# Dividing attention outputs by the softmax sums, and spreading the mLSTM's stabiliser rows by DMA: one encoder layer on one core

## The chip, the cores and the metric

One of the eight cores of a Trainium2 chip runs the kernel. The metric is the device time of one execution in microseconds (us); lower is better. The core has five engines, each with an instruction queue of its own: TensorE (PE, matmuls and transposes), VectorE (DVE), ScalarE (ACT), GpSimd (POOL) and SyncE (SP, which here only issues transfers, in order). Transfers themselves run on 16 DMA engines.

## What is computed

One layer of a hybrid encoder, applied to two groups of 512 tokens (width 1024) with shared weights. The parts that matter here:

```python
# mLSTM, per head and direction (stabiliser m_comb, one value per token)
m_comb = jnp.maximum(d_inter, jnp.max(d_intra, axis=-1))
w_intra = jnp.exp(d_intra - m_comb[..., None])
s = jnp.einsum('bhtd,bhsd->bhts', qb, kb) * w_intra
...
h = num / jnp.maximum(jnp.abs(den), jnp.exp(-m_comb))[..., None]
# attention, 8 heads
scale = (A_NOPE + A_ROPE) ** -0.5
s = jnp.einsum('bqhd,bkhd->bhqk', qn, k_nope) + jnp.einsum('bqhr,bkr->bhqk', qr, k_rope)
p = jax.nn.softmax(s.astype(jnp.float32) * scale, axis=-1).astype(v.dtype)
return jnp.einsum('bhqk,bkhd->bqhd', p, v)
```

Around them stand RMS norms, one input projection, merge gates, two branch projections, an output projection, a SwiGLU feed-forward part and a gated embedding.

## The kernel before

Activations lie transposed: 128 channels on the partitions, the 512 tokens of one group (g = 0, 1) along a row. Nearly every product is made of three matmuls of high and low parts (hi*hi, hi*lo, lo*hi); a tensor is split by a cast (ACT, line 158 or 168) and a subtraction (line 154). Weights come in by SP: load, split, use, through two buffers of each kind.

Order of the work: each engine has a queue, and a scheduler with a timing model chooses the order of the instructions from the code as it is written, by their dependences and free buffers. Some stretches are pinned to program order; those that the change touches are not. So a changed instruction can move others.

**The mLSTM stage** (about 80 to 490 us of the profile). A function `mlstm_proj` (line 515) makes queries, keys, values and output gates of a head; `mlstm_chain` (line 584) does one head and one group in two directions (d = 0, 1), 16 directions in all. The stabiliser, with sign turned, is kept for all 64 rows (direction, group, head) in `Mn`, one row of 512 tokens each; `nmr` stacks its high and low parts (lines 495 and 496). For one direction the row is needed on all 128 partitions: POOL casts a column of `esel` to a selection matrix `sel` (line 594), one matmul spreads the row into the PSUM bank `b0` (line 596), and two more make `b1`, the same with the causal mask added (lines 598 and 599). Ten Exp per direction (line 611) read blocks of `b0`, and of `b1` where the block lies on the diagonal, with a bias per partition. The result is multiplied by the scores (line 619) and split (lines 620 and 154); the products with the values (line 633) follow, then the division and the norm. Banks of PSUM in this stage: two for projections (`mm`), two for scores and products, two for transposes, two shared by `b0`, `b1` and another spread (`bc`).

**Merge gates** (line 695) and the values of attention (lines 720 to 734) follow, some gates also between heads of attention.

**Attention** (about 600 to 861 us): for each of 8 heads and 2 groups, `attn_proj` (line 773) makes the operands, reading the values `avt` from DRAM (line 787), and `attn` (line 791) works in four blocks of 128 queries. A block has five score matmuls (lines 799 to 803) into a bank of `sc` (three banks), the maximum over keys (DVE, line 805), its multiplication by -scale (DVE, line 806), Exp with that bias and the sum over keys as a second output (ACT, line 808), the sum's reciprocal (DVE, line 809), the normalising of p (line 811 on ACT for three blocks, line 813 on DVE for one), four transposes into a bank of `pt` (line 816, two banks), and the split of the result (line 818 on ACT, line 154 on DVE, into `aph` and `apl`). After the four blocks twelve matmuls with the values fill the one bank of `av` (lines 823 to 825); ACT copies it to `oz` (line 827, pool EV, tag "ch", two buffers), and SP stores it in DRAM (line 828).

**Hops**: between the last heads, the operands of the next stage (the projection of the mLSTM's outputs, lines 956 to 958) are loaded from DRAM (line 832), summed on POOL or DVE (lines 862 to 875, `ld`), and split (line 884 for the cast, `xh`). `HOPS` (line 1435) says how many units are written behind which head. When the last head begins, loads go to other buffers for a second pass of sums. The pool EV with tag "bk" (two buffers) holds the merge gates' rows `tg` and a part of the hops' loads.

**Behind 861 us**: branch projections, output projection, feed-forward and embedding, untouched by the change.

## Time and profile before

| | |
|---|---|
| runs | 1882.21, 1882.19, 1881.48 us |
| median of the runs | 1882.19 us |
| span of the profiled execution | 1884.6 us (2.4 us above the median) |
| TensorE, busy | 1846.2 us, 98% |
| VectorE, ScalarE, GpSimd, busy | 1234.4, 885.5, 374.5 us |
| granted TensorE clock, mean | 0.993 of full speed |

How rows are read: a group's row has line, engine, operation, out<-in by the program's names, shapes and count, then busy time in us and the mean of one in ns, then the idle time of the engine just before these instructions with what ended it. A row of the timeline begins with the start and the duration in us. "PE sc L799 <- ACT p L808: 4.5, 5, 2.4" means that TensorE, before the instruction of line 799, waited for ACT's line 808: 4.5 us in total, five times, 2.4 us at the longest. Matmuls are pipelined, so the records of two neighbours overlap; the distance between their starts is what one costs.

### The profile page before, as it was taken

How to read it: one execution, taken by the hardware profiler on the slowest of the kernel's cores; microseconds unless marked ns; L12 is line 12 of the kernel's file. 1: busy time of each engine (PE TensorE's matmuls, PEld its weight loads, DVE VectorE, ACT ScalarE, POOL GpSimd, SP SyncE). 2: the span in 40 equal slices, each digit the busy share in tenths (PEclk: the TensorE clock that was granted, in tenths of full speed). 3: DMA queues.
4: the chain of work that ended last, by engine and by line, in shares of the span. 5: the costliest groups of instructions: out<-in, count | busy, mean ns of one | idle time of the engine just before them, and what ended most of it. 6: DMA issues, size and time to landing. Idle time of an engine off the chain costs nothing.

```text
span 1884.6 us, 24479 instructions
## 1 busy us (share of the span) xinstructions
PE 1846.2 (98%) x8849; PEld 1535.3 (81%) x8849; DVE 1234.4 (66%) x2200; ACT 885.5 (47%) x1726; POOL 374.5 (20%) x281
## 2 busy tenths in 40 slices
PE   9999999999999999899999999999999999999996
PEld 7888898988887888677878888888888887888786
DVE  6747575836554667976897587444444568878756
ACT  6255465543444666775434355333433343434333
POOL 0000000100000000352050003665566523111000
PEclk9999999999999999999999999999999999999998
DMA  4111111112254222445565241332223346543332
GB/s 166 52 45 35 57 34 57 35 67 71 81 170 140 65 73 87 129 153 192 166 207 173 90 162 68 111 118 95 95 90 121 103 158 228 157 130 100 106 134 95
DMA packets 98377, 208.11 MB, mean 110 GB/s; under 512 B 10832, under 2 KB 21456, under 8 KB 98256
## 3 DMA queue, kind: packets, MB, share of 16 engines
q1 hardware_dynamic: 85600, 161.72, 25.8%
q10 hardware_dynamic: 12096, 43.00, 7.1%
q0 software_dynamic: 560, 1.84, 0.2%
q8 instruction: 69, 1.13, 0.2%
q14 instruction: 52, 0.43, 0.1%
HBM read 151.89 MB, written 54.10 MB: 109 GB/s over the span
## 4 chain that ended last, share of the span: by engine, by line
PE 85%; DVE 9%; DMA 3%; ACT 1%; issue 1%; SPq 0%; POOL 0%; ACTq 0%; DVEq 0%
PE b L956 13%; PE b L958 12%; PE b L957 12%; PE mm L183 7%; PE mm L185 7%; PE mm L184 7%; PE mm L79 3%; PE nm L633 3%; DVE xl L154 2%; PE mm L548 2%; PE mm L550 2%; PE mm L549 2%; PE pt L816 1%; PE mm L1322 1%; PE mm L1323 1%
## 5 line engine op out<-in xcount | busy, mean ns | idle before, releaser
L957 PE MATMUL b<-xl,wp 128*128 128x512 f32 x1148 | 448.1, 392 | 1.7 <-DVE xl L154 1.7
L956 PE MATMUL b<-xh,wp 128*128 128x512 f32 x1148 | 442.1, 393 | 6.6 <-ACT u L997 2.3
L958 PE MATMUL b<-xh,wp 128*128 128x512 f32 x1148 | 444.2, 392 | 0.4 <-DVE wp L154 0.4
L900 ACT CAST wp<-wst 128x512 fp32r<-128x512 f32 (+1 forms) x270 | 164.2, 612 | 307.3 <-PE b L958 258.9
L154 DVE TENSOR_TENSOR wp<-wst,wp 128x512 fp32r<-128x512 f32 (+1 forms) x270 | 235.6, 875 | 67.0 <-ACT wp L900 66.6
L956 PEld LDWEIGHTS b<-xh,wp 128*128 128x128 f32 x1148 | 216.1, 188 | 59.1 <-ACT wp L900 5.5
L957 PEld LDWEIGHTS b<-xl,wp 128*128 128x128 f32 x1148 | 216.0, 188 | 49.0 <-DVE xl L154 2.6
L958 PEld LDWEIGHTS b<-xh,wp 128*128 128x128 f32 x1148 | 215.8, 188 | 48.3 <-DVE wp L154 1.3
L183 PE MATMUL mm<-hh,whi 128*128 128x512 f32 x560 | 220.4, 394 | 0.6 <-ACT raw L79 0.3
L184 PE MATMUL mm<-hl,whi 128*128 128x512 f32 x560 | 219.5, 392 | 0.0
L185 PE MATMUL mm<-hh,wlo 128*128 128x512 f32 x560 | 219.3, 392 | 0.0
L1002 DVE TENSOR_TENSOR u<-b,u 128x512 f32<-128x512 f32 x90 | 61.7, 689 | 132.5 <-PE b L958 82.6
L168 ACT CAST whi<-wst 128x1024 fp32r<-128x1024 f32 (+1 forms) x69 | 71.0, 1029 | 114.4 <-PE mm L184 69.6
L183 PEld LDWEIGHTS mm<-hh,whi 128*128 128x128 f32 x560 | 105.6, 189 | 23.3 <-ACT raw L79 0.8
L185 PEld LDWEIGHTS mm<-hh,wlo 128*128 128x128 f32 x560 | 105.5, 188 | 21.9
L184 PEld LDWEIGHTS mm<-hl,whi 128*128 128x128 f32 x560 | 105.6, 189 | 21.4
L927 POOL TENSOR_TENSOR s<-wst,wst 128x512 f32<-128x512 f32 (+1 forms) x30 | 47.4, 1579 | 321.9 <-DMA wst<-w 87.3
L154 DVE TENSOR_TENSOR wlo<-wst,whi 128x1024 fp32r<-128x1024 f32 (+1 forms) x69 | 83.1, 1204 | 30.9 <-ACT whi L168 30.5
L997 ACT COPY u<-b 128x512 f32<-128x512 f32 x90 | 50.8, 589 | 98.0 <-PE b L958 70.7
L1220 POOL TENSOR_TENSOR sg<-sg,u 128x512 f32<-128x512 f32 x30 | 54.6, 1819 | 203.3 <-DVE u L1002 203.3
L154 DVE TENSOR_TENSOR xl<-ld,xh 128x512 fp32r<-128x512 f32 x121 | 89.1, 764 | 7.0 <-ACT xh L884 6.2
L154 POOL TENSOR_TENSOR vnl<-avt,vnh 128x512 fp32r<-128x512 f32 x16 | 21.2, 1322 | 309.9 <-ACT vnh L158 251.4
(357 smaller groups left out, 3621.4 us busy)
## 6 DMA issues: line engine op xcount, KB each, us to landing
wst<-w SPq DMA_DIRECT2D x73, 512.0 KB
wst<-w ACTq DMA_DIRECT2D x60, 512.0 KB
ld<-actd SPq DMA_DIRECT2D x77, 256.0 KB
actd<-t SPq DMA_DIRECT2D x40, 256.0 KB
x<-x SPq DMA_DIRECT2D x32, 256.0 KB
ld<-hzd SPq DMA_DIRECT2D x32, 256.0 KB
wst<-wd ACTq DMA_DIRECT2D x16, 512.0 KB
actd<-sg SPq DMA_DIRECT2D x30, 256.0 KB
```

Of the source, the lines that this page charges most:

```text
L79: r = f(*args, **kw)
L154: e.tensor_tensor(out=out, in0=src, in1=hi.bitcast(F32), op=ALU.subtract)
L168: S.copy(hi[:, :n], st[:, :n])
L183: E.matmul(bk, whi[:, c], hi, start=k == 0, stop=False)
L184: E.matmul(bk, whi[:, c], lo, start=False, stop=False)
L185: last_mm[0] = E.matmul(bk, wlo[:, c], hi, start=False, stop=k == nk - 1)
L633: E.matmul(bk, l, r, start=n == 0, stop=n == len(terms) - 1)
L900: S.copy(hi, src)
L956: E.matmul(bk, whi[:, c], hi, start=bool(first) and k == 0, stop=False, **sk)
L957: E.matmul(bk, whi[:, c], lo, start=False, stop=False, **sk)
L958: E.matmul(bk, wlo[:, c], hi, start=False, stop=k == self.kh - 1, **sk)
L1002: V.tensor_tensor(out=t, in0=b, in1=t, op=ALU.add if name == "P2" else ALU.subtract)
```

## The change

*mLSTM.* `nmr`, `esel`, `sel` and the three matmuls per direction go. `Mn` is written once to DRAM (`nmd`); for each direction SP loads one row of it, broadcast to 128 partitions, into `b0`, a buffer of pool EV with tag "bk" (256 KB); POOL adds the mask into `b1`, a buffer of pool MC (two). The Exps read SBUF in place of PSUM, the masks stay fp32, and one of the two `bc` banks becomes a third `mm` bank.

*Attention.* The scale goes into the norm of the query latent (`lat_norms`), the maximum comes out negated, and Exp takes it as its bias; lines 806, 811 and 813 go. The four sums of a head's blocks stand in one tile `den`; one reciprocal makes `rden` (128x4). That is written to DRAM transposed, in pieces of one element (`rsd`), read back broadcast to 128 partitions into `rb` (pool EV, tag "bk"), and POOL multiplies `oz` by it before it is stored. Probabilities stay undivided up to there.

By count, in the instruction queues: PE 48 fewer (the matmuls); DVE 132 fewer (64 scalings, 48 reciprocals, 16 normalising passes, 4 others); ACT 49 fewer (48 normalising passes and the cast of `nmr`); POOL 16 casts fewer, 16 additions and 16 multiplications more; SP 48 transfers more (16 `b0`, 16 `rsd`, 16 `rb`, one `nmd`, less `esel`).

```diff
@@ -129,7 +129,7 @@
     def bank(n="mm"):
         return pb[0](n)
 
-    banks("P1", dict(mm=2, sc=2, tp=2, bc=2), mm="mm", sc="sT nm", tp="ssc tpc vtp ht", bc="bc bd rbc")
+    banks("P1", dict(mm=3, sc=2, tp=2, bc=1), mm="mm", sc="sT nm", tp="ssc tpc vtp ht", bc="rbc")
 
     cols = cp.tile([P, NCOL], F32, name="cols")
     nc.sync.dma_start(cols, a["cols"])
@@ -282,7 +282,7 @@
-    MC = Slots("MC", sel=2)
+    MC = Slots("MC", b1=2)
@@ -402,22 +402,15 @@
     X0.close()
 
 
-    nmr = MC.pool.tile([P, T], F32R, name="nmr")
+    nmd = dr.tile([64, T], F32, name="nmd")
     mcols = [MC.pool.tile([P, 5, NB, 2, 4], F32, name=f"mcols{g}") for g in range(G)]
-    identr = MC.pool.tile([P, P], F32R, name="identr")
-    V.tensor_copy(out=identr, in_=ident)
     aug = MC.pool.tile([P, 2, NB, 2], F32, name="aug")
     GP.memset(aug, 0.0)
     GP.memset(aug[:, 0, :, 0:1], 1.0)
-    esel = MC.pool.tile([P, 64], F32, name="esel")
-    nc.sync.dma_start(esel, a["esel"])
-
     masks = []
     for d in range(2):
-        st = R("tr", "mst")
-        nc.sync.dma_start(st[:, 0:P], a["mask"][d])
-        m = MC.pool.tile([P, P], F32R, name=f"mask{d}")
-        V.tensor_copy(out=m, in_=st[:, 0:P])
+        m = MC.pool.tile([P, P], F32, name=f"mask{d}")
+        nc.sync.dma_start(m, a["mask"][d])
         masks.append(m)
 
     def row(n):
@@ -492,8 +485,7 @@
     V.tensor_scalar(out=M, in0=M, scalar1=-1.0, scalar2=None, op0=ALU.mult)
     Mn = row("Mn")
     flip(Mn, M)
-    S.copy(nmr[0:64], Mn)
-    V.tensor_tensor(out=nmr[64:128], in0=Mn, in1=nmr[0:64].bitcast(F32), op=ALU.subtract)
+    nc.sync.dma_start(nmd, Mn)
     for d in range(NB + 1):
         src = A[d] if d < NB else em
         fl = row("fl")
@@ -589,16 +581,13 @@
         dn = sm.tile([P, 2 * NB], F32, name=nm("dn"), tag="dn", bufs=2)
         rc = sm.tile([P, 2 * NB], F32, name=nm("rc"), tag="rc", bufs=2)
         for d in range(2):
-            sel = MC("sel", "sel", F32R, (P, P))
             rw = 32 * d + 4 * g + hd
-            GP.tensor_copy(out=sel, in_=esel[:, rw : rw + 1].to_broadcast([P, P]))
-            b0 = bank("bc")
-            E.matmul(b0, sel, nmr, start=True, stop=True)
-            b1 = bank("bd")
-            E.matmul(b1, sel, nmr, start=True, stop=False)
-            E.matmul(
-                b1.rearrange("p (a b) -> p a b", a=NB), identr, masks[d][:, None, :].to_broadcast([P, NB, P]),
-                start=False, stop=True,
+            b0 = EV("bk", "b0")
+            nc.sync.dma_start(b0, nmd[rw : rw + 1].to_broadcast([P, T]))
+            b1 = MC("b1", "b1")
+            GP.tensor_tensor(
+                out=b1.rearrange("p (a b) -> p a b", a=NB), in0=b0.rearrange("p (a b) -> p a b", a=NB),
+                in1=masks[d][:, None, :].to_broadcast([P, NB, P]), op=ALU.add,
             )
             w = M2("w", "w", F32, (P, 10 * P))
             phi = M2("ph", "ph", F32R, (P, 10 * P))
@@ -675,7 +664,9 @@
         r = rsqrt(ro, 32, 1.0 / 256)
         for j, (n, gn, g) in enumerate(pairs):
             c = slice(8 * j, 8 * j + 8)
-            V.tensor_tensor(out=r[:, c], in0=r[:, c], in1=rcol[g], op=ALU.mult)
+            V.scalar_tensor_tensor(
+                out=r[:, c], in0=r[:, c], scalar=SCALE if n == "cq" else 1.0, in1=rcol[g], op0=ALU.mult, op1=ALU.mult
+            )
             bc = spread(r[:, c], lambda: M1("tr", "diag", F32R))
             for i in range(2):
                 t = early[f"{n}{i}", g]
@@ -733,6 +724,7 @@
+    rsd = [[dr.tile([NB, P], F32, name=f"rsd{g}_{c}") for c in range(AH)] for g in range(G)]
@@ -767,7 +759,6 @@
-    scale = (128 + 64) ** -0.5
@@ -791,6 +782,7 @@
     def attn(hd, g, ops):
         (qh, ql), (nh, nl), (vh, vl), q2 = ops
         kh, kl = kst[g]
+        mx, den, rden = (sm.tile([P, NB], F32, name=nm(n), tag=n, bufs=2) for n in ("mx", "den", "rden"))
         ph = Q("ph", "aph", F32R, (P, NB, T))
         pl = Q("pl", "apl", F32R, (P, NB, T))
         for i in range(NB):
@@ -801,22 +793,19 @@
             E.matmul(bk, ql[:, c], nh, start=False, stop=False)
             E.matmul(bk, q2[:, c], kh, start=False, stop=False)
             E.matmul(bk, q2[:, c], kl, start=False, stop=True)
-            mx = sm.tile([P, 4], F32, name=nm("mx"), tag="mx", bufs=4)
-            V.tensor_reduce(out=mx[:, 0:1], in_=bk, axis=mybir.AxisListType.X, op=ALU.max)
-            V.tensor_scalar(out=mx[:, 1:2], in0=mx[:, 0:1], scalar1=-scale, scalar2=None, op0=ALU.mult)
+            V.tensor_reduce(out=mx[:, i : i + 1], in_=bk, axis=mybir.AxisListType.X, op=ALU.max, negate=True)
             p = Q("p", "p")
-            S.activation(out=p, in_=bk, func=AF.Exp, bias=mx[:, 1:2], scale=scale, accum_out=mx[:, 2:3])
-            V.reciprocal(out=mx[:, 3:4], in_=mx[:, 2:3])
-            if i != 1:
-                S.activation(out=p, in_=p, func=AF.Copy, scale=mx[:, 3:4])
-            else:
-                V.tensor_scalar(out=p, in0=p, scalar1=mx[:, 3:4], scalar2=None, op0=ALU.mult)
+            S.activation(out=p, in_=bk, func=AF.Exp, bias=mx[:, i : i + 1], accum_out=den[:, i : i + 1])
             tp = bank("pt")
             for j in range(NB):
                 E.transpose(tp[:, j * P : (j + 1) * P], p[:, j * P : (j + 1) * P], ident)
             tp3 = tp.rearrange("p (a b) -> p a b", a=NB)
             S.copy(ph[:, :, c], tp3)
             lo_of(pl[:, :, c], tp3, ph[:, :, c])
+        V.reciprocal(out=rden, in_=den)
+        nc.sync.dma_start(rsd[g][hd].rearrange("a p -> p a"), rden)
+        rb = EV("bk", "rb")
+        nc.sync.dma_start(rb, rsd[g][hd].rearrange("a p -> (a p)")[None, :].to_broadcast([P, T]))
         ob = bank("av")
         for j in range(NB):
             c = slice(j * P, (j + 1) * P)
@@ -825,6 +814,7 @@
             E.matmul(ob, vh[:, c], pl[:, j], start=False, stop=j == NB - 1)
         o = EV("ch", "oz")
         S.copy(o, ob)
+        GP.tensor_tensor(out=o, in0=o, in1=rb, op=ALU.mult)
         nc.sync.dma_start(ozd[g][hd], o)
 
     def load(src, sl=EV, tag="bk", n="ld"):
@@ -1431,6 +1421,7 @@
+SCALE = (128 + 64) ** -0.5
@@ -1502,12 +1493,11 @@
-    esel = (ar(P)[:, None] % 64 == ar(64)[None, :]).astype(f)
-        mask=mask, esel=esel,
+        mask=mask,
```

How the queues changed, in rows of the instruction order (line, operation, out<-in with buffer numbers, in square brackets the semaphores waited for). Lines of the changed kernel are some ten lower: L818 is the store of `oz` (L828 before), L806 and L808 are the transfers `rsd` and `rb`.

SP, at the third head, before:

```order
L828 DMA ozd_1_5715<-oz_6576 128x512 [waits DMAHW0_49,Activation_49]
L166 DMA wst_7378<-wa 128x768 [waits DMAHW2_49,DMAHW1_49,DVE_49]
L828 DMA ozd_2_5708<-oz_6793 128x512 [waits Activation_49]
L700 DMA tmd_7_4816<-tg_6956 128x512 [waits DMAHW3_49,Activation_49]
L700 DMA tmd_7_4824<-tg_6985 128x512 [waits DMAHW4_49,Activation_49]
L166 DMA wst_7674<-wa 128x768 [waits DMAHW7_49,DMAHW5_49,DVE_49]
L828 DMA ozd_2_5716<-oz_6919 128x512 [waits DMAHW6_49,Activation_49]
```

The same place in the changed kernel, where `rsd` is the write of the reciprocals and `rb` the read:

```order
L818 DMA ozd_1_5658<-oz_6502 128x512 [waits Pool_49]
L806 DMA rsd_2_5667<-rden_6627 128x4x1 [waits DMAHW1_49,DVE_49]
L808 DMA rb_6696<-rsd_2_5667 128x512 [waits DMAHW5_49,DMAHW6_49,DMAHW2_49,DMAHW1_49]
L166 DMA wst_7273<-wa 128x768 [waits DMAHW3_49,DVE_49]
L818 DMA ozd_2_5651<-oz_6711 128x512 [waits DMAHW4_49,Pool_49]
L806 DMA rsd_2_5675<-rden_6745 128x4x1 [waits DVE_49]
L808 DMA rb_6814<-rsd_2_5675 128x512 [waits DMAHW5_49]
L691 DMA tmd_7_4759<-tg_6867 128x512 [waits DMAHW7_49,Activation_49]
L818 DMA ozd_2_5659<-oz_6829 128x512 [waits DMAHW0_49,Pool_49]
```

Before each store of `oz` a pair of transfers now stands in the queue, the second of them waiting for the first to have landed, and the store waits for POOL where it waited for ACT. Weight loads (`wst`) and merge gates (`tmd`) stand behind them.

ACT, near the end of attention, before (`xh` are casts of hop operands, `aph` casts of transposed probabilities, `p` the Exps and normalising passes):

```order
L808 ACTIVATE p_7918,mx_7915<-sc_7909,mx_7915 128x512 [waits DVE_49,PE_49,Activation_49]
L884 CAST xh_8289<-ld_8284 128x512 [waits DVE_49]
L811 ACTIVATE p_7898<-p_7898,mx_7895 128x512 [waits DVE_49]
L811 ACTIVATE p_7918<-p_7918,mx_7915 128x512 [waits DVE_49]
L818 CAST aph_7847<-pt_7862 128x4x128 [waits PE_49]
L158 CAST knh_7984<-pj_7977 128x512
L884 CAST xh_8294<-ld_8284 128x512 [waits Pool_49]
L827 COPY oz_7775<-av_7762 128x512 [waits DMAHW5_49,PE_49]
L818 CAST aph_7847<-pt_7882 128x4x128 [waits PE_49]
L808 ACTIVATE p_8031,mx_8028<-sc_8022,mx_8028 128x512
L818 CAST aph_7847<-pt_7902 128x4x128 [waits PE_49]
```

and the place of the last hop operand's casts in the changed kernel (L874 is the hop cast, L803 that of the probabilities, L798 the Exp, L816 the copy of `oz`):

```order
L803 CAST aph_8152<-pt_8195 128x4x128 [waits PE_49]
L798 ACTIVATE p_8267,den_8240<-sc_8260,mx_8239 128x512 [waits DVE_49,Activation_49]
L874 CAST xh_8136<-ld_8131 128x512 [waits DVE_49]
L803 CAST aph_8152<-pt_8211 128x4x128 [waits PE_49]
L798 ACTIVATE p_8283,den_8240<-sc_8276,mx_8239 128x512 [waits Activation_49]
L798 ACTIVATE p_8299,den_8240<-sc_8292,mx_8239 128x512 [waits DVE_49,PE_49,Activation_49]
L874 CAST xh_8141<-ld_8131 128x512 [waits Pool_49]
L803 CAST aph_8242<-pt_8253 128x4x128 [waits DVE_49,PE_49]
L816 COPY oz_8235<-av_8222 128x512 [waits DMAHW1_49,PE_49]
L803 CAST aph_8242<-pt_8269 128x4x128 [waits PE_49]
L803 CAST aph_8242<-pt_8285 128x4x128 [waits PE_49]
L803 CAST aph_8242<-pt_8301 128x4x128 [waits PE_49]
```

The casts of the last hop operand of the first pass (`ld_8284` before, `ld_8131` now) stood amid the Exps of earlier attentions; now the second of them stands ahead of all four casts of the last attention, and waits for POOL.

POOL, where that operand is made, before (L865 is its sum, L868 the first sums of the second pass, `vnl` the low part of values):

```order
L865 TENSOR_TENSOR ld_8284<-ld_8284,ld_8146 128x512 [waits DMAHW1_49,DVE_49]
L154 TENSOR_TENSOR vnl_7992<-avt_7988,vnh_7990 128x512 [waits DMAHW4_49,Activation_49]
L154 TENSOR_TENSOR vnl_8144<-avt_8140,vnh_8142 128x512 [waits DMAHW5_49,DVE_49,Activation_49]
L868 TENSOR_TENSOR ld_8528<-ld_8528,ld_8530 128x512 [waits DMAHW5_49,DMAHW4_49]
L930 TENSOR_TENSOR wst_8644<-wst_8644,wst_8646 128x512 [waits DVE_49]
L868 TENSOR_TENSOR ld_8537<-ld_8537,ld_8539 128x512 [waits DMAHW7_49,DMAHW6_49]
L868 TENSOR_TENSOR ld_8546<-ld_8546,ld_8548 128x512 [waits DMAHW1_49,DMAHW0_49]
```

and in the changed kernel (L858 and L864/L865 are sums of the second pass, L817 the multiplication of `oz`, L855 the operand's sum):

```order
L864 TENSOR_TENSOR ld_8435<-ld_8435,ld_8359 128x512 [waits DMAHW4_49,Pool_49]
L817 TENSOR_TENSOR oz_7969<-oz_7969,rb_7954 128x512 [waits Activation_49]
L864 TENSOR_TENSOR ld_8445<-ld_8445,ld_8368 128x512 [waits DMAHW6_49,Pool_49]
L865 TENSOR_TENSOR ld_8435<-ld_8435,ld_8438 128x512 [waits DMAHW5_49,Pool_49]
L864 TENSOR_TENSOR ld_8455<-ld_8455,ld_8377 128x512 [waits DMAHW0_49]
L154 TENSOR_TENSOR vnl_8129<-avt_8125,vnh_8127 128x512 [waits Activation_49]
L865 TENSOR_TENSOR ld_8445<-ld_8445,ld_8448 128x512 [waits DMAHW7_49,Pool_49]
L864 TENSOR_TENSOR ld_8465<-ld_8465,ld_8386 128x512 [waits DMAHW2_49]
L865 TENSOR_TENSOR ld_8455<-ld_8455,ld_8458 128x512 [waits DMAHW1_49,Pool_49]
L817 TENSOR_TENSOR oz_8099<-oz_8099,rb_8084 128x512 [waits DMAHW3_49,Activation_49]
L865 TENSOR_TENSOR ld_8465<-ld_8465,ld_8468 128x512 [waits DMAHW4_49,Pool_49]
L855 TENSOR_TENSOR ld_8131<-ld_8131,ld_8001 128x512 [waits DVE_49]
```

The operand's sum stood ahead of the second pass; now it stands behind it, as the sixteenth row counted from the pass's first sum (which stands four rows above the ones shown), and two multiplications of `oz` stand between.

## The prediction

> **What bounds the kernel now.** I read the page first, then the busy time by stretch, then TensorE's own start times and waits.
>
> ```profile
> span 1884.6 us, 24479 instructions
> PE 1846.2 (98%) x8849; PEld 1535.3 (81%) x8849; DVE 1234.4 (66%) x2200; ACT 885.5 (47%) x1726; POOL 374.5 (20%) x281
> ```
>
> TensorE (PE) is busy 98% of the span: 38.4 us of it are idle. A change gains by taking matmuls away, or by filling those gaps. The stretches (busy time and count for each engine, then granted clock, DMA share, GB/s) say where each applies:
>
> ```profile
> core 0: us, PE busy (x) PEld busy (x) DVE busy (x) ACT busy (x) POOL busy (x), PEclk, DMA share, GB/s
> 90.00:480.00 390.00, 389.67 (x2296) 346.20 (x2295) 241.28 (x537) 204.66 (x487) 19.18 (x30) 1.00 0.15 50
> 600.00:750.00 150.00, 150.00 (x724) 124.22 (x723) 96.91 (x199) 88.99 (x175) 9.49 (x7) 1.00 0.23 74
> 750.00:775.00 25.00, 23.69 (x114) 18.75 (x113) 19.57 (x42) 18.59 (x38) 7.63 (x6) 1.00 0.47 147
> 775.00:800.00 25.00, 21.66 (x106) 17.25 (x104) 24.59 (x50) 20.10 (x42) 6.62 (x6) 1.00 0.33 101
> 800.00:825.00 25.00, 21.93 (x99) 17.05 (x98) 20.49 (x45) 17.22 (x37) 5.55 (x4) 0.93 0.21 70
> 825.00:850.00 25.00, 23.32 (x121) 18.64 (x120) 18.87 (x47) 20.48 (x44) 19.40 (x15) 1.00 0.65 232
> 850.00:862.00 12.00, 10.27 (x41) 7.32 (x41) 3.46 (x7) 5.76 (x13) 0.00 (x0) 0.86 0.06 22
> 862.00:1885.00 1023.00, 999.57 (x4421) 817.86 (x4419) 682.76 (x1004) 417.98 (x729) 299.48 (x190) 0.99 0.40 133
> ```
>
> The mLSTM (90 to 480) and the first part of attention (600 to 750, where other matmuls are mixed in) are TensorE's alone: 389.67 of 390 and 150.00 of 150. There only removed matmuls shorten anything, and work added elsewhere is free until it makes TensorE wait. The last heads of attention (750 to 862) are different: TensorE is idle 1.31+3.34+3.07+1.68+1.73 = 11.1 us, while VectorE (DVE) is busy 24.59 of 25 in one slice. The code of the stretch behind 862 is not changed.
>
> **The mLSTM: 48 matmuls removed.** Each of 16 directions (2 groups, 4 heads, 2 directions) loses three. The timeline of the first, and the group over all:
>
> ```profile
> 94.11 0.40 PE L596 MATMUL bc<-nmr,sel 128*128 128x512 f32 x1
> 94.35 0.40 PE L598 MATMUL bd<-nmr,sel 128*128 128x512 f32 x1
> 94.58 0.39 PE L599 MATMUL bd<-mask,identr 128*128 128x512 f32 x1
> 94.81 0.28 PE L548 MATMUL mm<-whi,hh 128*128 128x256 f32 x1
> L596 PE MATMUL bc<-nmr,sel 128*128 128x512 f32 x16 | 6.3, 396 | 0.0
> ```
>
> Matmuls are pipelined: the record is 0.396 long, but the next one starts 0.23 to 0.24 later. From 94.11 to 94.81 the three take 0.70 us; 16 x 0.70 = **-11.2 us**. By record lengths it would be 48 x 0.396 = 19.0; the start times speak against that, and it stays only as a far bound.
>
> In their place a broadcast load b0 (SP's queue) and a GpSimd addition b1 for each direction. It would be felt first in the first chain, which needs the row Mn written to DRAM and read back:
>
> ```profile
> L454 DVE COPY Mn<-M x1: 417/417/417, 73.9 to 73.9; 32x512 f32<-32x512 f32 x1
> 57.50 0.34 SPq L443 DMA_DIRECT2D lfd<-lf  x1
> 60.28 0.62 SPq L450 DMA_DIRECT2D rfn<-lfd  x2
> 63.66 0.41 DVE L453 COPY rf<-rfn 32x512 f32<-32x512 f32 x1 [3.85 <-DMA rfn<-lfd]
> ```
>
> A like round trip (lf to DRAM and back) took 60.28-57.50 = 2.8 us to the read's issue and 3.4 more to its use. Mn is ready at 74.3, and the matmuls that it fed stood at 94.11, so 20 us cover 2.8+3.4 and a GpSimd operation of 1.3 (row below); I take 0. Later loads of b0 queue behind weight loads whose buffers come free late:
>
> ```profile
> SPq L166 <- DVE wlo L154: 269.7, 44, 23.0
> ```
>
> (waiter <- releaser: total, times, longest). SP already stands up to 23 us at a weight load, waiting for its buffer, so it runs ahead of need. A b0 whose buffer waits for the exponentials of two chains earlier holds the weight loads behind it. The rows show no such wait; bounds 0 and, with 1 us lost in each direction, +16. I take 0, since TensorE stands at 389.67 of 390 with that queue, and leave the other end to a rival. The 16 additions at about 1.3 us (21 us) go to a GpSimd that is busy 19.18 of 390.
>
> **Attention: 64 scalings, 48 reciprocals and 64 normalising passes leave.** Two views of 750 to 865 and 750 to 862: the groups, and what TensorE waited for.
>
> ```profile
> L811 ACT ACTIVATE p<-p,mx 128x512 f32<-128x512 f32 x23 | 16.5, 741 | 6.3 <-DVE mx L809 3.6 <-DVE mx L806 2.7
> L813 DVE TENSOR_SCALAR p<-p,mx 128x512 f32<-128x512 f32 x7 | 4.7, 673 | 0.1
> L809 DVE RECIPROCAL mx<-mx 128x1 f32<-128x1 f32 x30 | 4.6, 156 | 0.6 <-ACT p L808 0.5
> L806 DVE TENSOR_SCALAR mx<-mx 128x1 f32<-128x1 f32 x30 | 4.2, 142 | 0.2
> PE sc L799 <- ACT p L808: 4.5, 5, 2.4
> PE av L825 <- DVE apl L154: 2.0, 1, 2.0
> PE pt L816 <- DVE apl L154: 1.9, 4, 0.7
> PE pj L183 <- DVE qnl L154: 1.9, 3, 0.9
> PE av L823 <- ACT aph L818: 0.7, 1, 0.7
> ```
>
> DVE loses 4.7 + 4.2 + three quarters of 4.6 = 12.4 of the 87.0 us that it is busy from 750 to 862, ACT 16.5 of 82.2. The same cuts before 750 are worth nothing: TensorE is at 150.00 of 150. After 750 the waits named are of the kind that a shorter backlog cures: scores wait for a bank that an Exp has not read yet (4.5), transposes and projections for DVE's queue (1.9 + 1.9), together 8.3. I take 5 of it, since 8.3 needs every one to end and DVE keeps 74.6 of 112 us.
>
> The tail has a second term: while TensorE waits, its clock drops.
>
> ```profile
> 856.49 0.52 PE L823 MATMUL av<-aph,vnh 128*128 128x512 f32 x1 [0.68 <-ACT aph L818]
> 858.24 0.63 PE L824 MATMUL av<-aph,vnl 128*128 128x512 f32 x1
> 860.32 0.40 PE L823 MATMUL av<-aph,vnh 128*128 128x512 f32 x1
> 854.87 0.59 ACT L818 CAST aph<-pt 128x512 fp32r<-128x512 f32 x1 [0.50 <-PE pt L816]
> ```
>
> Nine matmuls start between 856.49 and 860.32, 0.43 apart instead of 0.23: 9 x 0.20 = 1.8 us more. The waits in the tail are 2.0 + 0.7, so 4.5 could go. I take 2, because a new wait enters there. In the changed order ACT's cast of the last hop operand stands ahead of the last head's casts, and it waits for GpSimd's sixteenth operation, counted from the second pass's first sum:
>
> ```profile
> 829.93 1.75 POOL L868 TENSOR_TENSOR ld<-ld,ld 128x512 f32<-128x512 f32 x1
> 832.89 3.78 POOL L868 TENSOR_TENSOR ld<-ld,ld 128x512 f32<-128x512 f32 x3
> ```
>
> In this clock 829.93 + 16 x 1.26 (3.78 / 3) = 850.1, just ahead of the casts of the last head (854.87 above). If attention runs 5 us earlier and the loads do not, the cast is late by a few us. Attention then gives -5 - 2 = **-7**, bounds 0 and -(11.1 + 1.8) = -13, and this new wait **+1**, bounds 0 and +6 (16 operations at 1.6 instead of 1.26).
>
> The new work: 16 GpSimd multiplies, and DVE meets GpSimd in one place:
>
> ```profile
> 828.68 1.29 POOL L154 TENSOR_TENSOR vnl<-avt,vnh 128x512 fp32r<-128x512 f32 x1 [10.38 <-ACT vnh L158]
> 828.89 1.63 DVE L154 TENSOR_TENSOR wp<-wst,wp 128x512 fp32r<-128x512 f32 x1
> L79 DVE TENSOR_TENSOR wp<-wst,wp 128x512 fp32r<-128x512 f32 x10 | 6.5, 686 | 0.9 <-ACT wp L79 0.9
> 830.51 0.68 DVE L154 TENSOR_TENSOR apl<-pt,aph 128x512 fp32r<-128x512 f32 x1
> ```
>
> The same DVE subtraction takes 0.69 us alone and 1.63 while GpSimd works. Seven or eight multiplies of 1.3 us fall after 750; were DVE always in such an operation they would cost 8 x 0.9 = 7 us of DVE, but the low parts of the transposed probabilities read PSUM, and the one at 830.51 takes 0.68 beside GpSimd's sum of 829.93; so I take under 1 us of DVE, in a DVE that loses 12.4, and count 0. The Trainium skill (GPSIMD Engine Reference, Key points) says that GpSimd shares its SBUF interfaces with VectorE and contends with instructions that have two SBUF inputs; it speaks against moving multiplies to GpSimd, and these rows agree. By it alone the whole 7 us would count, attention would gain nothing, and the sum would be -11.2 + 1 = -10.2.
>
> The new transfers: each of 16 attentions writes its reciprocals as 4-byte pieces, reads them back, and SP waits for the write before it issues the read, with weight and value loads behind it. The nearest row is the round trip above, 2.8 us with 256-byte rows. I take 3 us per attention, hidden under SP's lead of up to 23 us. The Trainium skill (DMA: Bandwidth & Descriptors, Specifications) says that transfers below 512 bytes become read-modify-writes and miss the line rate; no run here shows 4-byte pieces, and the page gives no duration. The multiply itself is off TensorE's path: its output goes to DRAM and is read by the next stage.
>
> **Sum.** -11.2 - 7 + 1 = -17.2. Against the profiled execution's 1884.6 that is 1867.4. The median shown is 1882.19, 2.4 lower; so 1882.2 - 17.2 = **1865.0**.
>
> **Rivals.** About 0.2% (3.8 us) is what a measurement can tell from no change: faster is below 1878.4, slower above 1885.9.
>
> - *All of the attention waits go.* DVE at 24.59 of 25 speaks for it, the crowded end against. -11.2 - 12.9 = -24.1: 1858. Chance 0.15.
> - *Attention waits change their owner.* TensorE waits for GpSimd, for ACT's cast of the hop operand, or for a DVE that loses the 7 us above to GpSimd's multiplies; the crowded end speaks for it, DVE's 12.4 us against. Only the matmuls count, and +1 to +6: 1872 to 1877. Chance 0.21.
> - *Slower: SP is held by the reciprocals' round trip.* A head takes 262/16 = 16 us (600 to 862). If the 512 pieces land in over about 10 us instead of 2.8, SP's wait plus the read fills the head's time, and value and weight loads come late in every one. At a tenth of a head's time each, 16 x 1.6 = +26, attention's -7 is gone: 1882.2 - 11.2 + 26 = 1897. Against: 2.8 us in the row. Chance 0.08.
> - *The matmuls' saving does not arrive.* Chains wait for b0 or b1 instead, 1 us in each direction: 1865 + 16 = 1881. 20 us of cover speak against. Chance 0.05.
>
> The forecast has the rest, 0.51. Forecast and the first two rivals are faster (0.87, less 0.02 for the second one's upper end), the last one lies within 0.2%, the third is slower: 0.85, 0.07, 0.08. The range runs from a little below the first rival, for a part of the 19.0 bound, to the upper end of the second: 1855 to 1878.
>
> **What would show it.** In the changed profile, TensorE from 90 to 480 at 389 of 390 or more and the last mLSTM matmul about 11 us earlier; no wait on a b0 or b1; the last head's L823 of 860.32 at about 843; fewer than 6 us of TensorE idle in the last 110 us of attention; the last cast of a hop operand waiting under 2 us for GpSimd; a read of the reciprocals issued within 4 us of its write. The forecast is wrong if SP waits 10 us for that write, if TensorE shows a wait for GpSimd or SP of 5 us or more at attention's end, or if the stretch behind attention, whose code is untouched, changes length by over 3 us.

## The result, and the profile after

The changed kernel takes 1903.5 us (median of four runs, 1899.6 to 1905.8), the kernel before 1881.8: a ratio of 1.0118, interval 1.0102 to 1.0134. It is 22 us slower; 17 us faster were forecast. The page of the kernel after:

```profile
span 1904.0 us, 24351 instructions
PE 1835.9 (96%) x8801; PEld 1530.1 (80%) x8801; DVE 1224.4 (64%) x2068; ACT 860.2 (45%) x1677; POOL 414.6 (22%) x297
```

The work went as forecast: 48 matmuls fewer and 10 us less of busy TensorE, 25 us less of ACT, 40 us more of GpSimd. But TensorE is now idle 68 us instead of 38. The stretches of the kernel after (columns as in the prediction) say where:

```profile
90.00:480.00 390.00, 389.25 (x2333) 347.37 (x2332) 263.87 (x593) 217.79 (x519) 30.50 (x30) 1.00 0.18 62
600.00:750.00 150.00, 147.89 (x707) 120.97 (x706) 86.03 (x136) 72.77 (x151) 20.79 (x16) 1.00 0.28 82
750.00:775.00 25.00, 19.78 (x86) 14.86 (x85) 14.99 (x25) 12.84 (x30) 5.55 (x5) 0.93 0.35 106
775.00:800.00 25.00, 15.36 (x62) 11.71 (x61) 17.36 (x27) 9.00 (x21) 5.82 (x5) 0.80 0.26 53
825.00:850.00 25.00, 16.57 (x71) 13.09 (x70) 11.21 (x19) 11.45 (x25) 5.72 (x5) 0.80 0.51 145
```

The mLSTM runs as before, 389.25 of 390, with more matmuls inside. The late heads are where time is lost: in the three slices shown TensorE is busy 15 to 20 of 25 us, at a granted clock of 0.80 to 0.93, and VectorE, which was nearly full in one slice there (24.59 of 25), now idles too. So it is not work that holds TensorE up. The last matmul on the values (tile av; count, shortest/median/longest in ns, first to last start), in the kernel before and in the one after:

```profile
L825 PE MATMUL av<-apl,vnh x64: 389/392/780, 624.4 to 860.8; 128*128 128x512 f32 x64
```

```profile
L814 PE MATMUL av<-apl,vnh x64: 389/389/796, 610.9 to 889.3; 128*128 128x512 f32 x64
```

Attention begins 13.5 us earlier and ends 28.5 later. From there to the end of the span it is 1884.6 - 860.8 = 1023.8 us before and 1904.0 - 889.3 = 1014.7 after: 9.1 us shorter, in code that the change doesn't touch. Three things are thus to explain: 13 us won ahead of attention, 42 lost in it, 9 won behind it. (They add up to 19, the difference of the two profiled executions. The one of the kernel before, 1884.6, lies above all its measured times, 1877.3 to 1882.2, so some of the 9 may be its own.)

What waits in the late heads of the kernel after, from 745 to 905 us for TensorE and ACT, 600 to 905 for SP (waiter <- releaser: total, times, longest; to land is, for a transfer, the time from its issue to the signal that it is complete):

```profile
PE pt L801 <- DVE apl L154: 18.0, 7, 8.0
PE av L812 <- ACT aph L803: 6.6, 2, 5.9
PE sc L791 <- ACT p L798: 6.3, 4, 4.6
ACT xh L874 <- DMA ld<-hzd: 26.1, 5, 9.7
ACT xh L874 <- DVE ld L852: 15.8, 3, 7.7
ACT xh L874 <- POOL ld L855: 8.6, 2, 6.0
SPq L808 <- DMA rsd<-rden: 112.7, 13, 11.0
```

TensorE waits for ACT's and VectorE's casts of the probabilities; ACT itself waits 50 us for hop operands whose loads, or the sums made of them, are late; and SP waits 113 us for the write of the reciprocals (rsd) to land before it may issue their read (rb). One such chain, in rows of the three timelines:

```profile
772.20 0.37 SPq L806 DMA_DIRECT2D rsd<-rden  x1
782.06 0.32 SPq L808 DMA_DIRECT2D rb<-rsd  x1
782.90 0.42 SPq L822 DMA_DIRECT2D ld<-hzd  x1
787.97 0.62 ACT L874 CAST xh<-ld 128x512 fp32r<-128x512 f32 x1 [9.68 <-DMA ld<-hzd]
789.13 0.80 PE L812 MATMUL av<-aph,vnh 128*128 128x512 f32 x1 [5.91 <-ACT aph L803]
```

The write goes out at 772.20, its read only at 782.06 (9.9 us; over all 13 waits 112.7 / 13 = 8.7), a hop load behind it at 782.90; ACT stands 9.68 us at that load's cast, and the cast of the probabilities behind it in ACT's queue keeps TensorE 5.91 us. It looks like the prediction's third rival, SP held by the round trip. The experiments show that most of the loss comes without any such wait.

### The profile page after: what moved, and what is told of

The parts are those of the page before. It is cut to its first block, busy times and chain, and to the rows that moved or that the text cites. A ratio compares the mean times of both kernels' runs of the same rounds, so it can differ in the third digit from the quotient of the medians.

```text
span 1904.0 us, 24351 instructions
## 1 busy us (share of the span) xinstructions
PE 1835.9 (96%) x8801; PEld 1530.1 (80%) x8801; DVE 1224.4 (64%) x2068; ACT 860.2 (45%) x1677; POOL 414.6 (22%) x297
## 4 chain that ended last, share of the span: by engine, by line
PE 46%; DVE 5%; DMA 3%; issue 1%; ACT 1%; SPq 0%; ACTq 0%; DVEq 0%
PE b L946 12%; PE b L948 12%; PE b L947 12%; PE mm L79 2%; DMA ld<-hzd 2%; PE mm L185 1%; PE mm L184 1%; PE mm L183 1%; DVE xl L154 1%; DVE wp L154 1%; PE mm L1312 1%; PE mm L1313 1%; PE mm L1311 1%; DMA rsd<-rden 0%; DMA wst<-wd 0%
## 5 line engine op out<-in xcount | busy, mean ns | idle before, releaser
L154 DVE TENSOR_TENSOR wp<-wst,wp 128x512 fp32r<-128x512 f32 (+1 forms) x270 | 229.0, 850 | 70.9 <-ACT wp L890 70.8
```

The costliest lines, as they stand in the source:

```text
L154: e.tensor_tensor(out=out, in0=src, in1=hi.bitcast(F32), op=ALU.subtract)
```

## The experiments

**The two parts apart.** e1 has only the hunks of the mLSTM, e2 only those of attention.

> The mLSTM's part of the change alone, attention as before. Theory A (the mLSTM's matmuls are saved, and all of the loss lies in attention, where SP's queue is held by the landing of the reciprocals' 4-byte write, 9.0 us at the median in the changed kernel): about 11 to 13 us under the kernel before, 1869 to 1872 us. Theory C (the spreading by transfers costs as much as the matmuls did): within 4 us of the kernel before, 1878 to 1886 us.

(The 9.0 us there and below is the middle of the two landings that the view gives for rsd, 12.5 for a write and 5.5 for a read; SP's rows say 8.2 to 12.5 for the write.)

e1: 1871.1 us, 0.9943 of the kernel before (0.9927 to 0.9960): 10 us saved, theory A. Its last matmul on the values starts at 848.0 instead of 860.8.

> Attention's part of the change alone, the mLSTM as before. Theory A and theory B (attention loses through the multiplies on GpSimd, the shared buffers of the row rb and the changed order, whatever the write takes) alike: the changed kernel's loss of 22 us plus the mLSTM's saving of 11 to 12, so 1912 to 1918 us. Theory C: about 1900 us, as the whole change.

e2: 1928.9 us, 1.0252 (1.0237 to 1.0268). The loss is attention's, but with 48 us it is larger than the 32 that the whole change and e1 leave for it, and the time lies outside what either theory allowed (1912 to 1918). SP's wait for the write is longer there too:

```profile
SPq L819 <- DMA rsd<-rden: 130.3, 16, 10.2
```

against 112.7 in 13 waits. Why the parts don't add up stays open.

**Take the write away, or its small pieces.**

```diff
-        nc.sync.dma_start(rsd[g][hd].rearrange("a p -> p a"), rden)
         rb = EV("bk", "rb")
-        nc.sync.dma_start(rb, rsd[g][hd].rearrange("a p -> (a p)")[None, :].to_broadcast([P, T]))
+        nc.sync.dma_start(rb, a["cos"][0:1].to_broadcast([P, T]))
```

> The changed kernel without the write of the reciprocals: the row rb is loaded, broadcast, from a constant input of the same size, so SP waits for no landing, while the broadcast load, its buffer and GpSimd's multiply stay (attention is multiplied by a wrong row). Theory A: the wait of 113 us on SP goes, and with it the loss in attention; the time falls to the sum of the prediction, 1860 to 1870 us. Theory B: the load, the buffers and the multiplies are there as before, so 1893 us or more.

e3: 1866.3 us, 0.9916 (0.9900 to 0.9932). All of the loss goes with the write; load, buffer and multiplies stay and cost nothing that shows. Theory B falls.

```diff
-        nc.sync.dma_start(rsd[g][hd].rearrange("a p -> p a"), rden)
+        rt = bank("pt")
+        E.transpose(rt[0:NB, 0:P], rden, ident)
         rb = EV("bk", "rb")
+        V.tensor_copy(out=rb[0:NB, 0:P], in_=rt[0:NB, 0:P])
+        nc.sync.dma_start(rsd[g][hd], rb[0:NB, 0:P])
```

> The changed kernel with the reciprocals transposed on TensorE (one transpose of 128x4 per head and group, copied by VectorE) and written to DRAM as four rows of 512 bytes, then read back broadcast as before. The round trip stays, the 512 pieces of 4 bytes go. Theory A with the pieces as its cause: the write lands in 2 to 3 us as the stores of oz do (2.1 us), SP is held about 5 us per head and group instead of 9 to 13, and the time falls to 1865 to 1880 us. Theory A with the round trip itself as the cause, or theory B: 1893 us or more.

e4: 1863.3 us, 0.9906 (0.9891 to 0.9920). The round trip through DRAM is still there; with rows of 512 bytes it is harmless. This kernel is faster than both.

**SP's wait, or the pieces themselves?** e5 writes the 4-byte pieces as the changed kernel does, but loads rb as e3 does, so nothing waits for them.

> The changed kernel with the write of the reciprocals in 4-byte pieces kept, but read by nobody: the row rb is loaded from a constant input as in e3 (attention is multiplied by a wrong row). Theory A1 (the loss comes from SP standing at the read until the write has landed): no instruction waits for the landing any more, so the time is that of e3, 1862 to 1870 us. Theory A2 (the 512 small pieces slow the DMA engines for the other transfers): 1885 us or more.

e5: 1897.8 us, 1.0086 (1.0070 to 1.0102). Theory A1, mine up to here, falls: 31.5 of the 37 us between e3 and the changed kernel are there with no instruction waiting for the write. In e5's view of waits ACT and TensorE still stand:

```profile
PE pt L801 <- DVE apl L154: 15.8, 6, 7.1
ACT xh L874 <- DVE ld L852: 18.0, 4, 6.9
ACT xh L874 <- DMA ld<-hzd: 16.5, 5, 7.2
```

> The changed kernel with the read of the reciprocals (the broadcast load of rb) issued by GpSimd instead of SP; the write in 4-byte pieces stays on SP. GpSimd then waits for the landing, 9 us at the median, and SP goes on. Theory A1: SP's wait of 113 us goes, the hop loads are in time, and most of the loss goes: 1865 to 1880 us, the rest for GpSimd's sums that stand behind its wait. Theory A2, or a loss through the multiplies' own lateness: 1893 us or more.

The edit of e6 is one word, the load of rb on `nc.gpsimd` instead of `nc.sync`. It takes 1916.0 us, 1.0180 (1.0163 to 1.0198), slower than the whole change. It is no clean test of SP's wait, though: SP no longer waits for the write, but for GpSimd's multiplies, which are late behind GpSimd's own wait (30.1 us in the kernel after):

```profile
SPq L818 <- POOL oz L817: 105.2, 14, 13.0
```

So the verdict on A1 rests on e5.

> The changed kernel with the hop loads between the heads issued by ScalarE instead of SP, everything else as it was (the pair of transfers with its wait stays on SP). Theory A1 in its narrow form (what SP's wait delays is above all the hop loads, for which ScalarE's casts stand in its queue: 26 us of waits there): half or more of the loss goes, 1865 to 1885 us. Its rival (the value and weight loads behind SP's wait are what comes late): 1893 us or more.

e7 (the hop loads on `nc.scalar`): 1913.2 us, 1.0163 (1.0136 to 1.0189). No gain, so my narrow form of A1 is wrong, but its rival (value and weight loads behind SP's wait) is not shown by that either, for the loads are as late in ACT's own queue. Two of them, by the view of DMA issues (KB, us to landing): the first issued at 755.68, long after a write, the second at 816.50, 1.3 us behind one that SP issued at 815.20:

```profile
ld<-hzd ACTq DMA_DIRECT2D x1, 256.0 KB, 2.9
...
ld<-hzd ACTq DMA_DIRECT2D x1, 256.0 KB, 11.6
```

The write holds up transfers of ACT's queue too: 2.9 us becomes 11.6. The same kind of load on SP's queue, issued at 815.42 and 1.3 us behind a write in the kernel after, and one 1.7 us behind a write in e11 below, whose pieces lie apart:

```profile
ld<-hzd SPq DMA_DIRECT2D x1, 256.0 KB, 10.5
```

```profile
ld<-hzd SPq DMA_DIRECT2D x1, 256.0 KB, 2.7
```

> The kernel of e4 (rows of 512 bytes) with a second round trip put in: the four rows are read back from DRAM, written to a second place, and only then read broadcast. No 4-byte piece is left, but SP stands at three landings per head and group instead of one, estimated from the 2.1 us of a store and 5.5 of a load at 7 to 10 us. Theory A1: the loss comes back with the wait, 1880 to 1905 us. A theory by which small pieces as such are the cause: as e4, 1860 to 1868 us.

```diff
         nc.sync.dma_start(rsd[g][hd], rb[0:NB, 0:P])
-        nc.sync.dma_start(rb, rsd[g][hd].rearrange("a p -> (a p)")[None, :].to_broadcast([P, T]))
+        nc.sync.dma_start(rb[0:NB, P : 2 * P], rsd[g][hd])
+        nc.sync.dma_start(rs2d[g][hd], rb[0:NB, P : 2 * P])
+        nc.sync.dma_start(rb, rs2d[g][hd].rearrange("a p -> (a p)")[None, :].to_broadcast([P, T]))
```

e8: 1868.1 us, 0.9930 (0.9911 to 0.9949), 4.8 above e4. SP's three waits in e8:

```profile
SPq L814 <- DMA rs2d<-rb: 18.9, 15, 2.6
SPq L813 <- DMA rb<-rsd: 13.7, 13, 2.3
SPq L812 <- DMA rsd<-rb: 12.4, 13, 2.0
```

They are 45 us in all (e4: 14.8), less than I had set, so this is no full dose; but 30 us more of waiting came with about 5 us of time, no more.

**What about the pieces?** The kernel after, from 792 to 801 us: SP's rows, then the view of DMA (40 slices of 0.225 us, tenths busy), in which nothing else moves:

```profile
792.31 0.37 SPq L806 DMA_DIRECT2D rsd<-rden  x1
800.55 0.33 SPq L808 DMA_DIRECT2D rb<-rsd  x1
```

```profile
DMA  0000046000000000000000000000000000000000
DMA packets 528, 0.00 MB, mean 0 GB/s; under 512 B 528, under 2 KB 528, under 8 KB 528
```

All 528 packets are through by 793.6, and then the 16 engines show nothing for 7 us until the landing releases SP. By these records the time is neither the packets' own nor that of queueing behind other data. e9, e11, e13 and e14 are e5 with another layout in DRAM. The edit of e11 (e13 has `[NB, P, 16]`, e14 `[NB, P, 4]`; e9 writes `rden` as it is into `[P, NB]`):

```diff
-    rsd = [[dr.tile([NB, P], F32, name=f"rsd{g}_{c}") for c in range(AH)] for g in range(G)]
+    rsd = [[dr.tile([NB, P, P], F32, name=f"rsd{g}_{c}") for c in range(AH)] for g in range(G)]
-        nc.sync.dma_start(rsd[g][hd].rearrange("a p -> p a"), rden)
+        nc.sync.dma_start(rsd[g][hd][:, :, 0:1].rearrange("a p o -> p a o"), rden.rearrange("p (a o) -> p a o", o=1))
```

> As e5 (write kept but read by nobody, rb from a constant input), with the write not transposed: 128 pieces of 16 bytes instead of 512 of 4. Since e5 showed that the loss comes with the small pieces and not with SP's wait, theory D1 says that each piece costs the DMA engines a fixed time (about 9 us / 512): a quarter of the pieces lands in about 2 to 4 us, and the time is 1862 to 1874 us. Theory D2, that any such write shorter than the stores' rows blocks for its 8 to 9 us whatever the count: as e5, 1890 us or more.

> As e5, with the 512 pieces of 4 bytes put 512 bytes apart in DRAM (a buffer of 256 KB for each head and group). Theory D4 (neighbouring pieces lie in the same line of memory, and each write waits for the one before on that line): the pieces no longer meet, the write lands in 2 to 4 us, the time is 1862 to 1872 us. Theories D1 and D3 (a cost for each piece, whatever its neighbours): as e5, 1890 us or more.

> As e11, the 512 pieces of 4 bytes now 64 bytes apart instead of 512 (4 bytes in e5). If pieces meet in lines of 64 bytes or less, none meet: the write lands in about 2 us and the time is e11's, 1863 to 1872 us. If they meet in lines of 512 bytes (eight pieces in each), the landing and the time lie between e11 and e5: 4 us or more and 1872 us or more.

> As e11, the 512 pieces of 4 bytes 16 bytes apart. e9's 128 pieces of 16 bytes lay as near and landed in 1.4 us. If four pieces in 64 bytes are enough to meet, landing and time lie between e11 and e5: about 3 to 5 us, 1870 to 1885 us. If only pieces nearer than 16 bytes meet: 2 us and 1863 to 1872 us.

e9 (128 pieces of 16 bytes, side by side) 1867.9 us, 0.9923 (0.9905 to 0.9940); e11 1867.7, 0.9929 (0.9914 to 0.9944); e13 1868.9, 0.9926 (0.9909 to 0.9942); e14 1870.4, 0.9938 (0.9923 to 0.9953). The landings, one write that the trace could follow in each kernel (for the hop loads a median of a few), in the order e5, e14, e13, e11, e9:

```profile
rsd<-rden SPq DMA_DIRECT2D x16, 2.0 KB, 10.5
ld<-hzd SPq DMA_DIRECT2D x32, 256.0 KB, 11.5
```

```profile
rsd<-rden SPq DMA_DIRECT2D x16, 2.0 KB, 2.6
ld<-hzd SPq DMA_DIRECT2D x32, 256.0 KB, 4.6
```

```profile
rsd<-rden SPq DMA_DIRECT2D x16, 2.0 KB, 2.0
```

```profile
rsd<-rden SPq DMA_DIRECT2D x16, 2.0 KB, 2.0
ld<-hzd SPq DMA_DIRECT2D x32, 256.0 KB, 4.4
```

```profile
rsd<-rden SPq DMA_DIRECT2D x16, 2.0 KB, 1.4
```

e5 and e11 have the same instructions in the same order on every engine; only the addresses in DRAM differ. 512 pieces of 4 bytes land in 10.5 us when they lie side by side and in 2.0 when 64 or 512 bytes apart; even 16 bytes suffice for 2.6. So it is not the count or the size (D1 and D2 fall) but how densely the pieces lie, and the lost 30 us go with that. At 64 bytes apart nothing of it is left (e13 is as quick as e11); e5 has 16 pieces in 64 bytes, e9 and e14 have four and are nearly unharmed. Theory D4, that each piece waits for the one written before it in the same line of memory, fits, but no run looks inside. How long such a line is stays open too: pieces further apart are also fewer in any longer stretch (512, 128 and 32 of them in 2 KB in e5, e14 and e13), so e13 does not show that a line has 64 bytes, as its expectation would have it.

> The changed kernel with the 512 pieces of 4 bytes sent into SBUF (four transfers of 128 pieces, each into one row of rb) and from there to DRAM as four rows of 512 bytes, then read broadcast. The pieces stay and SP stands at one landing more. Theory D3 (small pieces are slow where they are written to DRAM): the time is near e8's, which has the same waits without pieces, 1864 to 1876 us. Theory D1 (a fixed time for each piece wherever it goes): the loss stays, 1890 us or more.

```diff
-        nc.sync.dma_start(rsd[g][hd].rearrange("a p -> p a"), rden)
         rb = EV("bk", "rb")
+        for i in range(NB):
+            nc.sync.dma_start(rb[i : i + 1, 0:P], rden[:, i : i + 1])
+        nc.sync.dma_start(rsd[g][hd], rb[0:NB, 0:P])
```

e10: 1866.5 us, 0.9926 (0.9908 to 0.9944). Side by side in SBUF the 4-byte pieces do no harm. D3 is half right: of the two places tried only DRAM is slow, but by e11 not every small piece there is. This repairs the change without TensorE.

**GpSimd's multiplies.** e12 is e4 with the division on VectorE.

> The kernel of e4 with the division by the sums made by VectorE on its way out of PSUM (one operation instead of ScalarE's copy and GpSimd's multiply). If the multiplies on GpSimd cost next to nothing, as the prediction's sum has it: within 4 us of e4, 1859 to 1867 us; the bank of av is then held until rb has landed, which could cost up to 10 us. If GpSimd's contention with VectorE takes the 7 us of the prediction's bound: 1857 us or less.

```diff
-        S.copy(o, ob)
-        GP.tensor_tensor(out=o, in0=o, in1=rb, op=ALU.mult)
+        V.tensor_tensor(out=o, in0=ob, in1=rb, op=ALU.mult)
```

e12: 1869.7 us, 0.9937 (0.9922 to 0.9952), 6 us over e4. Taking the multiplies off GpSimd in this way wins nothing. But e12 has a cost of its own, which its expectation named: VectorE stands 11.3 us, in five waits, for rb to land before it can divide, and the bank of av is held so long. What the multiplies cost VectorE is read from the traces instead: behind 750 us its operations that overlap a multiply are together 2.2 us longer in e3 and e11, and 2.7 in e4, than the shortest of their kind.

**The stretch behind attention.** A tile of 64 bytes that nobody uses, put into the kernel before, shifts what lies behind it in SBUF as the change does:

```diff
     sm = ctx.enter_context(tc.tile_pool(name="sm", bufs=1))
+    sm.tile([P, 16], F32, name="pad")
```

> The kernel before with one unused tile of 64 bytes per partition put into the pool of small tiles. The order on every engine stays, only the addresses of the tiles behind it in SBUF shift by 64 bytes, as the changed attention's small tiles shift them (six tiles in place of four). From the end of attention to the end of the span the kernel before and e1 take 1023.8 and 1021.6 us, and every kernel with the changed attention about 1005 to 1017, though the code there is the same; their matmuls of 512 columns start 227.0 ns apart on the mean, against 228.5 in the kernel before and e1. Theory E (the addresses do it): steps of 227 ns there, and 5 to 8 us off the time, 1873 to 1878 us. Its rival (the changed attention or its buffers do it in another way): no change, 1879 to 1885 us.

> The kernel of e4 with one buffer instead of two for the reciprocals' tile, which moves the tiles behind it 32 bytes down; the order stays but for two rows. Under theory E this may undo or better the steps of 227 ns: 1860 to 1870 us, either way; under its rival it is e4's time, 1861 to 1866 us.

e15: 1875.7 us, 0.9973 (0.9963 to 0.9982), as theory E had it; e16: 1873.3 us, 0.9965 (0.9953 to 0.9977), above both of its ranges. The group of the branch's middle matmul, in the kernel before, e15, e4 and e16:

```profile
L957 PE MATMUL b<-xl,wp 128*128 128x512 f32 x1148 | 448.1, 392 | 1.7 <-DVE xl L154 1.7
```

```profile
L958 PE MATMUL b<-xl,wp 128*128 128x512 f32 x1148 | 445.5, 389 | 0.7 <-DVE xl L155 0.7
```

```profile
L950 PE MATMUL b<-xl,wp 128*128 128x512 f32 x1148 | 445.5, 389 | 0.8 <-DVE xl L154 0.8
```

```profile
L950 PE MATMUL b<-xl,wp 128*128 128x512 f32 x1148 | 448.2, 392 | 0.9 <-DVE xl L154 0.9
```

The mean of 392 ns becomes 389 by a shift of 64 bytes with all instructions in place (e15), and 392 again by 32 bytes back (e16, 0.6% over e4 by the ratios). In the profiles the stretch behind attention takes 1023.8 us in the kernel before and 1013.9 in e15, 1016.9 in e4 and 1026.0 in e16: the shift by 64 bytes shortens it by 9.9, the 32 bytes back lengthen it by 9.1, with the same instructions in the same order on every engine. By the ratio of the times e15 wins 3.4 to 7.0 us in all. So theory E holds, and this part of the change's effect is an accident of addresses. It is not the whole length of that stretch: e7 and e8, whose matmuls start as close together as in e4, have 1022.9 and 1020.2 us there, outside the 1005 to 1017 that e15's expectation gives.

## Why the prediction was wrong

- **The step that failed** is the new transfers: "The nearest row is the round trip above, 2.8 us with 256-byte rows. I take 3 us per attention, hidden under SP's lead of up to 23 us." The write took 8.2 to 12.5 us to land, and SP's lead does not hide its harm, since loads issued near it, on SP's queue and on ACT's, are late as well. The prediction priced the write by the length of a wait; the price is what the write does to its neighbours: 31.5 of 37 us with no instruction waiting for it (e5 against e3). Without the harm the time comes out near the forecast of 1865 (e3, e10 and e11 lie at 1866 to 1868 us), but partly by luck, as the points on attention's relief and on the stretch behind it show.
- **The third rival** had the sign and nearly the time (1897 against 1903.5), at a chance of 0.08 and with the wrong mechanism. SP's hold was its price; by e8 30 us of hold cost 5, and by e5 five sixths of the loss come without any wait. Its point of decision, a landing over about 10 us, was met by five of the 16 writes, since a slow landing and late transfers go together here. The row with 256-byte pieces spoke for 2.8 us and said nothing of neighbours of 4 bytes; there the other end of the range was missing.
- **The Trainium skill's rule on small transfers** (DMA: Bandwidth & Descriptors, Specifications), which the prediction put beside the rows, pointed the right way. But size alone isn't it: the same 4 bytes 64 bytes apart land in 2.0 us.
- **The mLSTM's matmuls**: -11.2 forecast by the distance of starts, -10.0 measured (e1, interval -7.5 to -13.7). Right, and the sum by record lengths (19.0) is out. No matmul of the mLSTM waits for b0 or b1, as forecast.
- **Attention's relief**: -7 forecast. With the pieces harmless, the last matmul on the values, in e1, e3 and e4:

```profile
L814 PE MATMUL av<-apl,vnh x64: 387/392/628, 611.7 to 848.0; 128*128 128x512 f32 x64
```

```profile
L813 PE MATMUL av<-apl,vnh x64: 389/389/796, 608.1 to 848.7; 128*128 128x512 f32 x64
```

```profile
L817 PE MATMUL av<-apl,vnh x64: 387/393/504, 608.9 to 842.6; 128*128 128x512 f32 x64
```

  e1 has the old attention, e3 and e4 the new. Against e1 attention ends 0.7 us later in e3 and 5.4 earlier in e4. In the other kernels whose write does no harm its end lies between 1.4 us earlier (e8) and 3.1 later (e9, e13); e16, which has e4's transfers, ends it 3.2 earlier. Most show no relief, so this term was too large as well. The kernels also differ in the order of their instructions; what share that has stays open.
- **The tail's cast** behind GpSimd: +1 forecast, bounds 0 to 6. In the kernel after ACT waits 8.6 us for GpSimd at such casts, in a stretch where loads are late. In e3 and e11 the last of them, near 838 us, waits 2.8 us for GpSimd, but ACT's next cast of probabilities then waits 1.9 us for TensorE, so no cost to TensorE shows; in e4 the last one waits for nobody.
- **GpSimd and VectorE**: under 1 us of VectorE forecast and counted as 0; the overlaps above cost it 2.2 to 2.7 us, far from the 7 of the bound. The Trainium skill's rule on the shared interfaces (GPSIMD Engine Reference, Key points) shows in single operations: the longest xl beside a multiply in e3 takes 1.80 us, the shortest 0.67. Whether this is why attention's relief did not come is not shown.
- **The stretch behind attention** was held fixed and is 9.1 us shorter in the profile; a change of addresses alone does as much (e15). So the nearness of 1865 to e3, e10 and e11 is partly luck: an overrated relief was made good by an effect not foreseen. That change of length, and SP's wait for the write (11.0 us at the longest), were among the prediction's signs of being wrong.

## What to carry to other kernels

Before a transposing transfer is put into a loop, look at where its pieces land: here 512 pieces of 4 bytes side by side in DRAM took 8.2 to 12.5 us to land, and made loads of two queues late whether or not anybody waited for the write. Transpose on chip (e4), go through SBUF (e10), or space the pieces (e11, e13 and e14, which were not read back here). When a wait on a queue looks like the cause, try the same transfer with nobody waiting for it; and when code that was not touched changes its time, look at whether its tiles have moved.

## What the runs showed of the hardware

- 512 pieces of 4 bytes written to DRAM land in 10.5 us (12.5 in the kernel after) side by side, 2.6 at 16 bytes apart, 2.0 at 64 and at 512; 128 pieces of 16 bytes side by side in 1.4 (one write followed in each kernel). In the write at 792.31 the packets' records end within 1.3 us of the issue; the rest shows only as silence.
- A load of 256 KB issued 1.3 us behind such a write, by another queue, landed after 11.6 us (e7); one issued 20.5 us behind the last write after 2.9 (e7), one 1.7 us behind a write with its pieces apart after 2.7 (e11).
- The mean record of a matmul of 512 columns behind attention was 392 or 389 ns by where its tiles lay in SBUF: shifted by 64 bytes (the kernel before to e15) or 32 (e4 to e16), worth 3.4 to 7.0 us of this kernel (e15). Which operand and which boundary it is stays open.
